# Queries and keys of retention heads 2 to 4 as seven half-width products, and retention's angle tables made a stage later

## The chip, the cores and the metric

The kernel runs on one core of a Trainium2 chip. The metric is device time in microseconds, from the start of the program to the end of its last instruction on the core. Times before are from three runs; the profile is one further execution, recorded by the hardware profiler.

## The reference

One layer of a decoder trunk, float32, batch 1, 512 positions, model width 1024. What matters here:

```python
h = rms_norm(x, norm_mix)
proj = h @ w_in
rq, rk, rv, rg, cq, ckv, krope, gr, gm = jnp.split(proj, offsets, axis=-1)

rq = rope(rq.reshape(B, S, RET_HEADS, RET_QK_DIM), pos)
rk = rope(rk.reshape(B, S, RET_HEADS, RET_QK_DIM), pos) * (RET_QK_DIM ** -0.5)
rv = rv.reshape(B, S, RET_HEADS, RET_V_DIM)
ro = retention(rq, rk, rv)
ro = rms_norm(ro, ret_norm.reshape(RET_HEADS, RET_V_DIM)).reshape(B, S, RET_V_W)
a_ret = (ro * jax.nn.silu(rg)) @ w_br
...
mo = causal_block_attention(q, k, v).reshape(B, S, MLA_V_W)
a_mla = mo @ w_bm
mixed = jax.nn.sigmoid(gr) * a_ret + jax.nn.sigmoid(gm) * a_mla
x = x + mixed @ w_o
```

Retention has 4 heads with queries and keys of 256 and values of 512 columns; `rope` turns each head's query and key by position: with the first 128 and last 128 of its columns called x1 and x2 it gives x1 cos - x2 sin and x2 cos + x1 sin. Cosine and sine depend on position and column alone and are one pair of 128 x 512 tables for all four heads. The other branch is latent attention with 8 heads. After `mixed @ w_o` come an MLP of width 4096 and a gated embedding, which the change doesn't touch.

## The kernel before

**Products.** Everything is held transposed: 128 channels on the partitions, 512 positions along the free axis. A product in float32 is made of three matmuls in a reduced format (`mm3`, L290 to L295): each operand is split into a high half `h` (a copy on ScalarE, rounded) and a low half `l` (VectorE, the rest), and low x high, high x low and high x high are added up in PSUM. All matmuls are recorded at one line, L167, so the profile's names tell them apart: `rq` and `rk` are the query and key products, `rv` and `rg` value and gate, `bm` the attention branch's output, `br` the retention branch's.

**Weights** come in chunks of 128 x 1024 (512 KB). SyncE issues the load into one of 6 raw tiles (`wr_...`), ScalarE makes the high half `wh_...` (L260), VectorE the low half `wl_...` (L264). There are 3 buffers for each half, so the halves of a chunk can be made only when TensorE has done the chunk three before it. One chunk is converted ahead of its use.

**Seven products for eight.** Values and gates are made two heads at a time by a scheme that multiplies two 2 x 2 block matrices with seven block products in place of eight. The blocks are halves of the depth (2 x 512 channels) and of positions (2 x 256) on the one side, halves of the depth and the two heads on the other. Its seven products have numbers 1, 7, 2, 6, 5, 4, 3. The activations' sums and differences, `XS[p]`, are made once (`x_operand`, tiles `sx`, `sy` and halves such as `s60h`). The sums and differences of weights are made by transfers: the fifth and seventh product's raw tile is loaded, and a second chunk is added to it by an accumulating transfer that GpSimd issues; the sixth and fourth product's is made in the seventh's tile by a further accumulating transfer each. `seven_out` puts the result together: a ScalarE copy out of PSUM after products 1, 7 and 6, a VectorE addition after 2, 5 and 4, and product 3 is the last block itself.

**Queries and keys** are made by `ret_qk` for each head separately: two chunks for the query and two for the key, each 8 x 3 matmuls with 512 columns and 128 output channels. After each, two VectorE products with the tables (512 columns each), after the second a difference and a sum, then the split in halves (`rqx`, `rqy`, `rkx`, `rky`).

**Tables.** Retention's are made early in the attention stage, between the statistics of the first pair of heads and the first head's factor: `ret_angles` (nine VectorE instructions on `tra` and `trk`, L466 to L477) and `ret_sincos` (two Sin and a Square on ScalarE, L485 to L487, and one VectorE instruction, L488), with the positions as loaded at the start.

**Order.** The steps of the kernel are a list, written out by hand. TensorE does them in that order. The framework's scheduler places the instructions of VectorE and ScalarE among those of earlier and later steps; each engine then works through its own list strictly in order. Heads go in pairs. In a pair: the first head's query and key, values and gates of both heads in seven products each, scores and attention of the first head, then (`ret_gated`, `ret_turned`, `branch_r`) its output times gate, 16 transposes on TensorE (`ot`), whose results are split in the halves `rog..h` (ScalarE, L308) and `rog..l` (VectorE, L311), and the branch product `br` from these. In the profile's names heads count from 0: `rog02l` is the low half of block 2 of the first head. The first head's `br` works on four blocks for each of its outputs; a first chunk of the second head's key stood between `ot` and `br`.

Of the kernel before, what the change touches and what calls it, by code (L numbers as in the profile page):

```python
# [37 lines left out]
P = 128  # L38
S = 512
# [12 lines left out]

C_ID, C_MASK, C_IND, C_INVR, C_INVM, C_SGN, C_N = 0, 128, 256, 260, 261, 262, 263

NDYN, NKEEP, NW, NRAW, NDRAW, AHEAD, PREP, EARLY, PAD = 45, 16, 3, 6, 4, 1, 3, 5, 104
GROUPS = DFF // 1024


# [12 lines left out]
def chunk_specs():  # L71
# [30 lines left out]
        for key, name in (("bm", "w_bm"), ("o", "w_o"), ("pg", "w_ple_gate")):  # L102
            add((key, n), name, full, _rng(n * P, P))
    for h in range(RH):
        for key, o in (("rq", O_RQ), ("rk", O_RK)):
            for n in range(2):
                add((key, h, n), "w_in", full, _rng(o + h * RQK + n * P, P))
        for k in range(4):
            add(("br", h, k), "w_br", _rng(h * RV, RV), _rng(2 * k * P, 2 * P))

    for kb in range(2):
        for fb in range(2):
            for q in range(RH // 2):
# [33 lines left out]
def trunk_layer(ctx: ExitStack, tc: tile.TileContext, xT, pT, pos, gains, const, decay, wstream, outT):  # L147
# [314 lines left out]


    def trig(name, posf, inv):
        ang, kf, c_, s_ = T(name + "a"), T(name + "k"), T(name + "c"), T(name + "s")
        TS(ang, posf, inv, None, op0=ALU.mult)  # L466
# [10 lines left out]
        TS(ang, ang, 3.1415925, -3.1415925, op0=ALU.min, op1=ALU.max)  # L477
        return ang, c_, s_
# [12 lines left out]
    def angles():  # L491
        posf = T("posf")
        nc.vector.tensor_copy(posf, posi)
        V["posf"] = posf
        V["am"] = trig("tm", posf, cst[:, C_INVM:C_INVM + 1])

    def tables():
        V["cm"], V["sn"] = sincos(*V["am"])

    def ret_angles():  # L500
        V["ar"] = trig("tr", V["posf"], cst[:, C_INVR:C_INVR + 1])

    def ret_sincos():
        V["cr"], V["sr"] = sincos(*V["ar"])
# [239 lines left out]
    def seven_out(c, p, ps, name):  # L744

        if p in (1, 7, 6):
            to = {1: 11, 7: 22, 6: 21}[p]
            c[to] = (T if to == 21 or name[0] == "c" else Z)(f"{name}{to}")
            ACT(c[to], ps, AF.Copy, scale=1.0 if p == 7 else -1.0)
            return None  # L750
        if p == 3:
# [53 lines left out]
    def ret_qk(w, h, key, n):  # L805
# [5 lines left out]
        if n == 0:  # L811
            d[key] = (a, b)
        else:
            a0, b0 = d[key]
            TT(a0, a0, a, op=ALU.subtract)
# [389 lines left out]
    for n in range(8):  # L1205
        step(("bm", n), branch_m, n)
        if n < 6:
            step(None, norm_x, 2 + n)
        if n == 3:
            step(None, x_operand, 7)  # L1210
    for p in (1, 2, 4):
        step(None, x_operand, p)
    def qk(h, key, n):
        step((key, h, n), ret_qk, h, key, n)

    def branch(h, *ks):
        for k in ks if h >= 0 else ():
            step(("br", h, k), branch_r, h, k)

    for q in range(RH // 2):  # L1220
        h = 2 * q
        qk(h, "rq", 0)
        qk(h, "rq", 1)
        if q:
            step(None, ret_turned, h - 1)
        qk(h, "rk", 0)
        branch(h - 1, 0)
        qk(h, "rk", 1)
        branch(h - 1, 1)
        for kind in ("rv", "rg"):  # L1230

            for p in (1, 7, 2, 6, 5, 4, 3):
                for c in range(2):
                    step(("sw", (kind, q), p, c), ret_seven, kind, q, p, c)
                if (kind, q) == ("rv", 0) and p in (1, 7, 2):
                    step(None, x_operand, {1: 6, 7: 5, 2: 3}[p])
                if (kind, p) == ("rv", 1):
                    branch(h - 1, 2)
                    if q:
                        step(None, ret_scores, h)  # L1240
                elif (kind, p) == ("rv", 6):
                    branch(h - 1, 3)
                    if not q:
                        step(None, ret_scores, h)
                elif (kind, p) == ("rg", 1):
                    step(None, ret_attend, h)
                elif (kind, p) == ("rg", 6):
                    qk(h + 1, "rq", 0)
                elif (kind, p) == ("rg", 4):
                    step(None, ret_gated, h)  # L1250
        qk(h + 1, "rq", 1)
# [131 lines left out]
```

## Time and profile before

| | us |
|---|---|
| median of 3 runs | 1105.74 (1105.18 to 1105.89) |
| the profiled execution | 1106.31 |
| its span | 1104.5 |
| TensorE busy | 1093.7 |
| VectorE busy | 711.1 |
| ScalarE busy | 541.1 |
| GpSimd busy | 89.9 |

The span is from the first to the last instruction that the profiler recorded. PE is TensorE, DVE VectorE, ACT ScalarE, POOL GpSimd, SP SyncE. A matmul's recorded duration overlaps with the next one's, so distances between starts tell what it takes. A row of the timeline has the start, the duration, engine, line, operation, output and inputs, shapes; a square bracket at its end tells the engine's idle time just before and what ended it. A row of the waits tells who waited for whom: total us, times, longest. A row of transfers ends with the median us from issue to landing.

### The profile page before, as it was taken

Reading aid. Unit: us, or ns where it says so; the run is one execution under the profiler, and the core shown is the slowest. Engines: PE = TensorE matmul, PEld = TensorE weight load, DVE = VectorE, ACT = ScalarE, POOL = GpSimd, SP = SyncE. Lnnn points to the kernel's source line nnn. Section 1 sums busy time; section 2 is a strip of 40 time slices with the busy share of each in tenths; the row PEclk is TensorE's granted clock in tenths of the full one; section 3 lists DMA queues with packets and bytes.
Section 4 is the critical chain, followed back from the end, with each engine's and each line's share of the span. In section 5 each row is a group of like instructions: output and inputs, shape, how many; then the busy total and the mean of one; then the engine's idle time right before and its main releaser. Section 6 shows DMA issues by size and latency. Waiting matters only on the chain.

```text
span 1104.5 us, 13845 instructions
## 1 busy us (share of the span) xinstructions
PE 1093.7 (99%) x5137; PEld 910.8 (82%) x5137; DVE 711.1 (64%) x1135; ACT 541.1 (49%) x785; POOL 89.9 (8%) x121
## 2 busy tenths in 40 slices
PE   9999999999999999999999999999999999999998
PEld 6778888888888888888888887888888888888887
DVE  7697677556774654656465577555556656658685
ACT  7647556444456545355654634434544444445542
POOL 0000000001111001121100100010100100101000
PEclk9999999999999999999999999999999999999999
DMA  7242231366789635488864944693765765738511
GB/s 258 72 120 87 72 106 54 128 208 205 207 194 246 195 143 171 116 202 205 209 207 115 268 142 158 193 276 103 181 172 150 184 182 136 190 116 219 147 54 58
DMA packets 59860, 178.02 MB, mean 161 GB/s; under 512 B 7376, under 2 KB 8784, under 8 KB 59536
## 3 DMA queue, kind: packets, MB, share of 16 engines
q1 hardware_dynamic: 45168, 129.66, 34.6%
q0 software_dynamic: 14480, 47.46, 21.6%
q8 instruction: 40, 0.66, 0.2%
q14 instruction: 28, 0.23, 0.1%
q10 hardware_dynamic: 144, 0.03, 0.0%
HBM read 157.97 MB, written 17.04 MB: 158 GB/s over the span
## 4 chain that ended last, share of the span: by engine, by line
PE 92%; DVE 4%; ACT 1%; issue 1%; DMA 1%; SPq 0%; DVEq 0%; ACTq 0%
PE up L167 16%; PE dn L167 14%; PE rv L167 7%; PE rg L167 7%; PE br L167 6%; PE pg L167 4%; PE gr L167 4%; PE rk L167 4%; PE bm L167 4%; PE rq L167 4%; PE wo L167 4%; PE gm L167 3%; PE ro L167 2%; PE sc L167 2%; PE pcq L167 1%; PE rs L167 1%
## 5 line engine op out<-in xcount | busy, mean ns | idle before, releaser
L167 PE MATMUL dn<-wh_dn,cl 128*128 128x512 f32 x224 | 87.2, 389 | 0.0
L167 PE MATMUL dn<-wh_dn,ch 128*128 128x512 f32 x224 | 87.1, 389 | 0.0
L167 PE MATMUL dn<-wl_dn,ch 128*128 128x512 f32 x224 | 87.1, 389 | 0.0
L260 ACT ACTIVATE wh_dn<-wr_dn 128x1024 fp32r<-128x1024 f32 x32 | 34.0, 1062 | 75.4 <-PE up L167 54.3
L260 ACT ACTIVATE wh_up<-wr_up 128x1024 fp32r<-128x1024 f32 x32 | 33.9, 1061 | 57.7 <-PE up L167 29.3
L264 DVE TENSOR_TENSOR wl_dn<-wr_dn,wh_dn 128x1024 fp32r<-128x1024 f32 x32 | 39.0, 1220 | 27.5 <-ACT wh_dn L260 27.5
L264 DVE TENSOR_TENSOR wl_up<-wr_up,wh_up 128x1024 fp32r<-128x1024 f32 x32 | 39.1, 1222 | 18.6 <-ACT wh_up L260 18.6
L167 PEld LDWEIGHTS dn<-wh_dn,cl 128*128 128x128 f32 x224 | 42.0, 188 | 8.8
L167 PEld LDWEIGHTS dn<-wh_dn,ch 128*128 128x128 f32 x224 | 42.0, 188 | 8.7
L982 DVE SCALAR_TENSOR_TENSOR f<-up,bcx 128x512 f32<-128x512 f32 x32 | 20.6, 685 | 44.4 <-PE up L167 44.4
L167 PEld LDWEIGHTS dn<-wl_dn,ch 128*128 128x128 f32 x224 | 42.0, 188 | 8.6
L260 ACT ACTIVATE wh_dn<-dr_dn 128x1024 fp32r<-128x1024 f32 x24 | 25.4, 1060 | 42.5 <-PE up L167 29.4
L260 ACT ACTIVATE wh_rg<-wr_rg 128x1024 fp32r<-128x1024 f32 x28 | 29.6, 1059 | 31.1 <-PE rg L167 12.1
L260 ACT ACTIVATE wh_rv<-wr_rv 128x1024 fp32r<-128x1024 f32 x28 | 29.6, 1058 | 30.6 <-PE rv L167 11.0
L222 POOL DMA_DIRECT2D dr_dn<-wstream x24 | 21.1, 890 | 289.4 <-DMA dr_dn<-wstream 165.0
L264 DVE TENSOR_TENSOR wl_dn<-dr_dn,wh_dn 128x1024 fp32r<-128x1024 f32 x24 | 29.3, 1222 | 22.4 <-ACT wh_dn L260 22.4
L264 DVE TENSOR_TENSOR wl_rg<-wr_rg,wh_rg 128x1024 fp32r<-128x1024 f32 x20 | 24.5, 1226 | 23.6 <-ACT wh_rg L260 23.6
L264 DVE TENSOR_TENSOR wl_rv<-wr_rv,wh_rv 128x1024 fp32r<-128x1024 f32 x20 | 24.4, 1223 | 18.0 <-ACT wh_rv L260 18.0
L1040 DVE TENSOR_TENSOR d<-d,dn 128x1024 f32<-128x1024 f32 x24 | 29.2, 1219 | 6.5 <-PE dn L167 6.5
L264 DVE TENSOR_TENSOR wl_br<-wr_br,wh_br 128x1024 fp32r<-128x1024 f32 x16 | 19.5, 1221 | 19.3 <-ACT wh_br L260 19.3
L260 ACT ACTIVATE wh_br<-wr_br 128x1024 fp32r<-128x1024 f32 x16 | 16.9, 1059 | 21.0 <-issue 12.8
L871 ACT ACTIVATE rt<-br 128x512 f32<-128x512 f32 x24 | 13.9, 593 | 25.9 <-PE br L167 25.9
(1819 smaller groups left out, 3440.7 us busy)
## 6 DMA issues: line engine op xcount, KB each, us to landing
wr_up<-wstream SPq DMA_DIRECT2D x32, 512.0 KB, 4.1
wr_dn<-wstream SPq DMA_DIRECT2D x32, 512.0 KB, 3.4
dr_dn<-wstream POOLq DMA_DIRECT2D x24, 512.0 KB, 7.6
wr_rv<-wstream SPq DMA_DIRECT2D x20, 512.0 KB, 4.4
wr_rg<-wstream SPq DMA_DIRECT2D x20, 512.0 KB, 5.3
wr_rv<-wstream POOLq DMA_DIRECT2D x16, 512.0 KB, 6.3
wr_rg<-wstream POOLq DMA_DIRECT2D x16, 512.0 KB, 7.4
wr_br<-wstream SPq DMA_DIRECT2D x16, 512.0 KB, 3.9
```

What stands on the lines that cost most here:

```text
L167: return tc.keep_in_program_order(nc.tensor.matmul(*a, **k))
L222: nc.gpsimd.dma_start(raw, chunk(("w", blk, kb, fb, c)), accum_op=ALU.add)
L260: i = ACT(hi, raw, AF.Copy, scale=sign)
L264: TT(lo, raw, hi.bitcast(F32), op=ALU.subtract)
L871: ACT(t, ps, AF.Copy)
L982: STT(u[:, i], ps[:, i], 0.0, V["bcx2"], op0=ALU.max, op1=ALU.mult)
L1040: TT(to, to, dps[p], op=ALU.add if sign > 0 else ALU.subtract)
```

## The change

Two things are changed.

First, queries and keys of the heads 1, 2 and 3 (heads 2 to 4 counted from one) are made by the scheme of seven as well: the two "columns" of the block matrix are now the head's query and key, 256 channels each. A product is 4 depth blocks x 2 output halves x 3 = 24 matmuls with 256 columns, with the weights as the stationary operand and `XS[p]` as the moving one. So a head has seven weight chunks of 24 short matmuls where it had four of 24 long ones, 5 plain and 4 accumulating loads where it had 4 plain ones, and the rotation is done in blocks of 256 positions (`ret_qk7`): per block one VectorE product of 512 columns and four operations of 256. Head 0 stays as it was. Steps are in a new order: the second head's seven products are spread among the gate products, and the last three stand before `ret_turned`; then both branch steps of the first head follow directly.

Second, `ret_angles` and `ret_sincos` move from the attention stage to that of `branch_m`, after its third and fifth output, with the positions loaded once more. The tables stand in one tile, `tab`. The pool of work tiles has 43 in place of 45.

```diff
-        for key, o in (("rq", O_RQ), ("rk", O_RK)):
+        for key, o in (("rq", O_RQ), ("rk", O_RK)) if h == 0 else ():
...
+            for h in range(1, RH):
+                add(("w", ("qk", h), kb, fb, 0), "w_in", _rng(kb * S, S), _rng((O_RQ, O_RK)[fb] + h * RQK, RQK))
...
     def ret_angles():
-        V["ar"] = trig("tr", V["posf"], cst[:, C_INVR:C_INVR + 1])
+        again, posf = dyn.tile([P, S], I32, tag="t", name="posr"), T("posrf")
+        nc.sync.dma_start(again, pos.partition_broadcast(P))
+        nc.vector.tensor_copy(posf, again)
+        V["ar"] = trig("tr", posf, cst[:, C_INVR:C_INVR + 1])
...
+    def ret_qk7(w, h, p):
+
+        ch, d = CHAIN[p], R[h]
+        if p in (1, 7, 2):
+            qkps[ch] = B(f"qk{h}{p}")
+        ps = qkps[ch]
+        for o in range(2):
+            for k in range(4):
+                mm3(ps[:, o * 256:o * 256 + 256], cut(w, k * 256 + o * P), XS[p][k], p in (1, 7, 2) and o + k == 0,
+                    o == 1 and k == 3, skip_group_check=True)
+        done = seven_out(d.setdefault("qk", {}), p, ps, f"qk{h}_")
+        if not done:
+            return
+        blk, t = done
+        key, cs = ("rq", "rk")[blk % 10 - 1], slice(256 * (blk // 10 - 1), 256 * (blk // 10))
+        a, b = T(f"{key}a{h}{blk}"), T(f"{key}b{h}{blk}")
+        lo_, hi_ = slice(0, 256), slice(256, 512)
+        TT(a.rearrange("p (k c) -> p k c", k=2), t.rearrange("p (k c) -> p k c", k=2), V["tab"][:, :, cs], op=ALU.mult)
+        TT(b[:, lo_], t[:, lo_], V["tab"][:, 1, cs], op=ALU.mult)
+        TT(b[:, hi_], t[:, hi_], V["tab"][:, 0, cs], op=ALU.mult)
+        first = key not in d
+        if first:
+            d[key] = (T(f"{key}u{h}"), T(f"{key}v{h}"))
+        u, v = d[key]
+        TT(u[:, cs], a[:, lo_], a[:, hi_], op=ALU.subtract)
+        TT(v[:, cs], b[:, lo_], b[:, hi_], op=ALU.add)
+        if not first:
+            d[key] = (split(u, f"{key}x{h}"), split(v, f"{key}y{h}"))
...
-    step(None, ret_angles)
-    step(None, ret_sincos)
     step(None, head_factor, 0)
...
+        if n in (2, 4):
+            step(None, ret_angles if n == 2 else ret_sincos)
...
+        if q:
+            qk(h, 1, 7, 2, 6)
+            step(None, ret_turned, h - 1)
+            qk(h, 5)
+            branch(h - 1, 0)
+            qk(h, 4, 3)
+            branch(h - 1, 1)
...
+        seven("rg", q, 7, 2, 6)
+        qk(h + 1, 1, 7)
+        seven("rg", q, 5)
+        qk(h + 1, 2)
+        seven("rg", q, 4)
+        step(None, ret_gated, h)
+        qk(h + 1, 6)
+        seven("rg", q, 3)
+        qk(h + 1, 5, 4, 3)
         step(None, ret_turned, h)
-        qk(h + 1, "rk", 0)
-        branch(h, 0)
-        qk(h + 1, "rk", 1)
-        branch(h, 1)
+        branch(h, 0, 1)
         step(None, ret_scores, h + 1)
```

Two places show what the change does to the engines' own lists. The first is VectorE around the transposes `ot` and the branch product `br` of head 0. In these names `z` and `o` are gate and output, `wl_...` a low half of weights, `rog00l` to `rog03l` the low halves that `br` multiplies, and `rqa`, `rqb`, `rqu`, `rqv`, `rka`, `rkb`, `rku`, `rkv` steps of the rotation. Before:

```order
L264 TENSOR_TENSOR wl_br_0_3991<-wr_br_0_3988,wh_br_0_3990 128x1024
L809 TENSOR_TENSOR rqa_3938<-rq_3913,trs 128x512
L810 TENSOR_TENSOR rqb_3939<-rq_3913,trc 128x512
L815 TENSOR_TENSOR rqa_3784<-rqa_3784,rqa_3938 128x512
L816 TENSOR_TENSOR rqb_3785<-rqb_3785,rqb_3939 128x512
L311 SCALAR_TENSOR_TENSOR rog00l<-ot_3952,gn,rog00h 128x512
L306 TENSOR_TENSOR rqx1l<-rqa_3784,rqx1h 128x512
L311 SCALAR_TENSOR_TENSOR rog01l<-ot_3961,gn,rog01h 128x512
L306 TENSOR_TENSOR rqy1l<-rqb_3785,rqy1h 128x512
L264 TENSOR_TENSOR wl_rk_1_4026<-wr_rk_1_4023,wh_rk_1_4025 128x1024
L311 SCALAR_TENSOR_TENSOR rog02l<-ot_3970,gn,rog02h 128x512
L311 SCALAR_TENSOR_TENSOR rog03l<-ot_3979,gn,rog03h 128x512
```

After, from the first weight half of `br` on; ahead of it stand, since the fifth of head 1's products, `qk_22`'s sum and its rotation (six rows as from `qk_21` to `rqv` here):

```order
L266 TENSOR_TENSOR wl_br_0_4103<-wr_br_0_4100,wh_br_0_4102 128x1024
L763 TENSOR_TENSOR qk_21_3977<-qk_21_3977,qk_3797 128x512
L266 TENSOR_TENSOR wl_br_1_4184<-wr_br_1_4181,wh_br_1_4183 128x1024
L847 TENSOR_TENSOR rqa_4085<-qk_21_3977,tab 128x512
L848 TENSOR_TENSOR rqb_4086<-qk_21_3977,tab 128x256
L849 TENSOR_TENSOR rqb_4086<-qk_21_3977,tab 128x256
L854 TENSOR_TENSOR rqu_3898<-rqa_4085 128x256
L855 TENSOR_TENSOR rqv_3899<-rqb_4086 128x256
L313 SCALAR_TENSOR_TENSOR rog00l<-ot_4145,gn,rog00h 128x512
L308 TENSOR_TENSOR rqx1l<-rqu_3898,rqx1h 128x512
```

and on to the fourth block:

```order
L313 SCALAR_TENSOR_TENSOR rog01l<-ot_4154,gn,rog01h 128x512
L308 TENSOR_TENSOR rqy1l<-rqv_3899,rqy1h 128x512
L847 TENSOR_TENSOR rka_4130<-qk_3764,tab 128x512
L848 TENSOR_TENSOR rkb_4131<-qk_3764,tab 128x256
L849 TENSOR_TENSOR rkb_4131<-qk_3764,tab 128x256
L854 TENSOR_TENSOR rku_4052<-rka_4130 128x256
L855 TENSOR_TENSOR rkv_4053<-rkb_4131 128x256
L266 TENSOR_TENSOR wl_br_2_4224<-wr_br_2_4221,wh_br_2_4223 128x1024
L308 TENSOR_TENSOR rkx1l<-rku_4052,rkx1h 128x512
L308 TENSOR_TENSOR rky1l<-rkv_4053,rky1h 128x512
L313 SCALAR_TENSOR_TENSOR rog02l<-ot_4163,gn,rog02h 128x512
L313 SCALAR_TENSOR_TENSOR rog03l<-ot_4172,gn,rog03h 128x512
```

Between `rog01l` and `rog03l` stood one row of the query, one of weights and `rog02l`; now the key's last rotation, a chunk of weights and both key splits stand there too.

The second place is ScalarE in front of retention's first query product, which multiplies `xn0` to `xn7` (`gb` is the other branch's gate, a Sigmoid; `s60h` and `s61h` belong to `XS[6]`). Before:

```order
L260 ACTIVATE wh_rq_1_2970<-wr_rq_1_2968 128x1024
L305 ACTIVATE s60h<-sx_2792 128x512
L305 ACTIVATE xn6h<-xr_2843 128x512
L696 ACTIVATE gb_2856<-gb_2856 128x512
L260 ACTIVATE wh_rk_0_3005<-wr_rk_0_3003 128x1024
L305 ACTIVATE xn7h<-xr_2887 128x512
L305 ACTIVATE s61h<-sx_2793 128x512
```

After:

```order
L262 ACTIVATE wh_rk_0_3008<-wr_rk_0_3006 128x1024
L307 ACTIVATE xn6h<-xr_2842 128x512
L492 ACT_TABLE_LOAD
L492 ACTIVATE tab<-tra 128x512
L493 ACTIVATE tab<-tra 128x512
L494 ACTIVATE tab<-tab 128x512
L705 ACT_TABLE_LOAD
L705 ACTIVATE gb_2859<-gb_2859 128x512
L307 ACTIVATE xn7h<-xr_2890 128x512
L307 ACTIVATE s61h<-sx_2792 128x512
```

`xn6h` stood before the key's weight half and stands behind it now, and the two Sins, the Square and two table loads stand between it and `xn7h`.

More of the change, by code (lines that the diff above doesn't have):

```diff
@@ L53 @@
 C_ID, C_MASK, C_IND, C_INVR, C_INVM, C_SGN, C_N = 0, 128, 256, 260, 261, 262, 263
-NDYN, NKEEP, NW, NRAW, NDRAW, AHEAD, PREP, EARLY, PAD = 45, 16, 3, 6, 4, 1, 3, 5, 104
+NDYN, NKEEP, NW, NRAW, NDRAW, AHEAD, PREP, EARLY, PAD = 43, 16, 3, 6, 4, 1, 3, 5, 104
 GROUPS = DFF // 1024
@@ L464, in trig @@
     def trig(name, posf, inv):
-        ang, kf, c_, s_ = T(name + "a"), T(name + "k"), T(name + "c"), T(name + "s")
+        ang, kf = T(name + "a"), T(name + "k")
+        if name == "tr":
+            V["tab"] = dyn.tile([P, 2, S], F32, tag="tab", name="tab", bufs=1)
+            c_, s_ = V["tab"][:, 0], V["tab"][:, 1]
+        else:
+            c_, s_ = T(name + "c"), T(name + "s")
         TS(ang, posf, inv, None, op0=ALU.mult)
@@ L493, in angles @@
         nc.vector.tensor_copy(posf, posi)
-        V["posf"] = posf
         V["am"] = trig("tm", posf, cst[:, C_INVM:C_INVM + 1])
@@ L747, in seven_out @@
             to = {1: 11, 7: 22, 6: 21}[p]
-            c[to] = (T if to == 21 or name[0] == "c" else Z)(f"{name}{to}")
+            c[to] = (Z if to != 21 and name[0] == "z" else T)(f"{name}{to}")
             ACT(c[to], ps, AF.Copy, scale=1.0 if p == 7 else -1.0)
@@ L817, in ret_qk @@
             d[key] = (split(a0, f"{key}x{h}"), split(b0, f"{key}y{h}"))
+    qkps = {}
+    def ret_qk7(w, h, p):
[25 more added lines that the diff above has]
+            d[key] = (split(u, f"{key}x{h}"), split(v, f"{key}y{h}"))
     def ret_scores(h):
@@ L1212, in trunk_layer, with qk, seven @@
         step(None, x_operand, p)
-    def qk(h, key, n):
-        step((key, h, n), ret_qk, h, key, n)
+    def qk(h, *ps):
+        for p in ps:
+            step(("sw", ("qk", h), p, 0), ret_qk7, h, p)
+    def seven(kind, q, *ps):
+        for p in ps:
+            for c in range(2):
+                step(("sw", (kind, q), p, c), ret_seven, kind, q, p, c)
     def branch(h, *ks):
-        for k in ks if h >= 0 else ():
+        for k in ks:
             step(("br", h, k), branch_r, h, k)
@@ L1221, in trunk_layer @@
         h = 2 * q
-        qk(h, "rq", 0)
-        qk(h, "rq", 1)
         if q:
+            qk(h, 1, 7, 2, 6)
             step(None, ret_turned, h - 1)
[L1226 to L1251, printed above, removed]
+            qk(h, 5)
+            branch(h - 1, 0)
+            qk(h, 4, 3)
+            branch(h - 1, 1)
+            seven("rv", q, 1)
+            branch(h - 1, 2)
+            step(None, ret_scores, h)
+            seven("rv", q, 7, 2, 6)
+            branch(h - 1, 3)
+        else:
+            for key in ("rq", "rk"):
+                for n in range(2):
+                    step((key, h, n), ret_qk, h, key, n)
+            for p, x in ((1, 6), (7, 5), (2, 3)):
+                seven("rv", q, p)
+                step(None, x_operand, x)
+            seven("rv", q, 6)
+            step(None, ret_scores, h)
+        seven("rv", q, 5, 4, 3)
+        seven("rg", q, 1)
+        step(None, ret_attend, h)
+        seven("rg", q, 7, 2, 6)
[7 more added lines that the diff above has]
+        qk(h + 1, 5, 4, 3)
         step(None, ret_turned, h)
-        qk(h + 1, "rk", 0)
-        branch(h, 0)
-        qk(h + 1, "rk", 1)
-        branch(h, 1)
+        branch(h, 0, 1)
         step(None, ret_scores, h + 1)
```

## The prediction

> **What bounds the kernel now.** I read the page first: busy time by engine and the chain of work that ended last.
>
> ```profile
> PE 1093.7 (99%) x5137; PEld 910.8 (82%) x5137; DVE 711.1 (64%) x1135; ACT 541.1 (49%) x785; POOL 89.9 (8%) x121
> ...
> PE 92%; DVE 4%; ACT 1%; issue 1%; DMA 1%; SPq 0%; DVEq 0%; ACTq 0%
> ```
>
> TensorE is busy for 1093.7 of the span's 1104.5 us. So the time changes in two ways only: TensorE gets less work, or it gets (or loses) stalls. The next view, the busy time between 204 and 667 us (from the end of attention through retention, where nearly all of the change lies), shows a TensorE without a gap; the waits of TensorE show that what stalls there are lie elsewhere. Four of them are of this change's first place, the attention stage:
>
> ```profile
> 204.00:667.00 463.00, 463.00 (x2132) 387.19 (x2131) 281.97 (x422) 230.94 (x346) 56.89 (x76) 1.00 0.67 187
> ```
>
> ```profile
> PE sc L167 <- ACT sqk L525: 0.8, 1, 0.8
> PE gm L167 <- DVE mx L642: 0.6, 1, 0.6
> PE pt0a L167 <- DVE p L651: 0.6, 1, 0.6
> ```
>
> The first row's columns are the stretch, its length, the busy time of PE, PEld, DVE, ACT and POOL, the granted clock (1.00) and the DMA share (0.67). In retention VectorE is busy for 282 of 463 us and ScalarE for 231: they have room in the mean. What counts is whether they are late at one moment.
>
> **Term 1, fewer cycles on TensorE.** Per head 4 chunks of 24 products over 512 columns become 7 chunks of 24 over 256. The timeline gives the distance between starts of both kinds: the first and the 25th matmul of `rq`, and 13 starts of the last gate product, which has 256 columns.
>
> ```profile
> 275.18 0.39 PE L167 MATMUL rq<-xn0h,wl_rq 128*128 128x512 f32 x1
> ...
> 280.62 0.39 PE L167 MATMUL rq<-xn0h,wl_rq 128*128 128x512 f32 x1
> ```
>
> ```profile
> 1097.06 0.28 PE L167 MATMUL pg<-x3g0h,wl_pg 128*128 128x256 f32 x1
> ...
> 1098.50 0.28 PE L167 MATMUL pg<-x3g4h,wl_pg 128*128 128x256 f32 x1
> ```
>
> (280.62 - 275.18)/24 = 0.227 us, and (1098.50 - 1097.06)/12 = 0.120 us, each with its own weight load. A head costs 96 x 0.227 = 21.8 us now and 168 x 0.120 = 20.2 us after: -1.6 us, not the -12.5% that seven for eight suggests, since the shorter matmul loses more of its time between two. Three heads: **-4.9 us**. Bounds: 0, if each of the 504 short ones started 0.01 us later than these rows have it, and -4.9, which I take. [...]
>
> **Term 2, the angle block leaves the attention stage.** Nine VectorE instructions and three of ScalarE stand between head 0's scores and their softmax:
>
> ```profile
> 83.82 0.48 DVE L466 TENSOR_SCALAR tra<-posf,cst 128x512 f32<-128x512 f32 x1
> ...
> 88.63 0.43 DVE L477 TENSOR_SCALAR tra<-tra 128x512 f32<-128x512 f32 x1
> 90.77 0.29 DVE L642 CUSTOM_DVE_ANT_0 p<-sc,kf 128x128 f32<-128x128 f32 x1 [1.70 <-ACT kf L611]
> ```
>
> ```profile
> 89.10 0.63 ACT L485 ACTIVATE trs<-tra 128x512 f32<-128x512 f32 x1 [5.21 <-DVE tra L477]
> ...
> 90.16 0.58 ACT L611 ACTIVATE kf<-pbk 128x512 f32<-128x512 f32 x1
> ```
>
> `kf`, on which the maximum at 90.77 waits, stands on ScalarE behind the Sin of 89.10. Without the block the softmax is 3 to 4 us earlier, and the waits of `sc`, `gm` and `pt0a` above, 0.8 + 0.6 + 0.6 = 2.0 us, lose their cause. Bounds: -2.0 and 0; in the changed order the low half of the next gate chunk stands behind `k3l`, a wait that can take some of it back. I take **-1.1**, about the middle.
>
> **Term 3, the angle block arrives in front of retention.** Its nine VectorE instructions go between those of the other branch's stage, whose VectorE is half idle; they cost nothing while TensorE's operands stay ahead. The ScalarE part does not fit so well. It brings two table loads (Sin, and Sigmoid back), and the order puts table, Sin, Sin, Square, table and a Sigmoid between `xn6h` and `xn7h`, the last operand of retention's first product. Now:
>
> ```profile
> 240.44 1.28 ACT L696 ACT_TABLE_LOAD   x1
> 241.74 0.63 ACT L696 ACTIVATE gb<-gb 128x512 f32<-128x512 f32 x1
> ...
> 271.47 0.62 ACT L305 ACTIVATE xn6h<-xr 128x512 fp32r<-128x512 f32 x1
> 271.99 0.61 ACT L696 ACTIVATE gb<-gb 128x512 f32<-128x512 f32 x1
> 275.43 1.06 ACT L260 ACTIVATE wh_rk<-wr_rk 128x1024 fp32r<-128x1024 f32 x1 [2.83 <-PE bm L167]
> 276.40 0.61 ACT L305 ACTIVATE xn7h<-xr 128x512 fp32r<-128x512 f32 x1
> ```
>
> ```profile
> 277.67 0.68 DVE L306 TENSOR_TENSOR xn7l<-xr,xn7h 128x512 fp32r<-128x512 f32 x1
> ```
>
> ```profile
> 280.16 0.39 PE L167 MATMUL rq<-xn7l,wh_rq 128*128 128x512 f32 x1
> ```
>
> `xn7l` ends at 278.35, and TensorE takes it at 280.16: 1.8 us of cover. After, `wh_rk` still starts at 275.43 (it waits for the last `bm` product), and `xn6h` now stands behind it, to 277.0. Then table 1.28, two Sins (the second 0.52 after the first), Square, table 1.28, Sigmoid: 276.9 -> 278.2 -> 279.9 -> 281.2 -> 281.8, so `xn7h` ends at about 282.4 and `xn7l`, with a product of VectorE before it, at 283.2. TensorE wants it at 280.16: **+3.0 us** (2 if the ScalarE starts overlap better, 4 if VectorE's own queue there, five instructions, comes on top).
>
> **Term 4, the transposed output of heads 1 and 3 is wanted at once.** Now a whole `rk` chunk lies between the transposes `ot` and the branch product `br`, which needs all four of `rog0`..`rog3`:
>
> ```profile
> 394.66 1.91 PE L167 MATMUL ot<-cst,o 128*128 128x128 f32 x16
> 396.32 0.48 PE L167 MATMUL rk<-xn0h,wl_rk 128*128 128x512 f32 x1
> ...
> 401.86 0.39 PE L167 MATMUL br<-rog00h,wl_br 128*128 128x512 f32 x1
> ```
>
> ```profile
> 395.47 0.68 DVE L810 TENSOR_TENSOR rqb<-rq,trc 128x512 f32<-128x512 f32 x1
> 396.06 0.68 DVE L815 TENSOR_TENSOR rqa<-rqa,rqa 128x512 f32<-128x512 f32 x1
> ...
> 397.26 0.74 DVE L311 SCALAR_TENSOR_TENSOR rog00l<-ot,gn,rog00h 128x512 fp32r<-128x512 f32 x1
> ...
> 399.79 1.22 DVE L264 TENSOR_TENSOR wl_rk<-wr_rk,wh_rk 128x1024 fp32r<-128x1024 f32 x1
> 400.92 0.74 DVE L311 SCALAR_TENSOR_TENSOR rog02l<-ot,gn,rog02h 128x512 fp32r<-128x512 f32 x1
> 401.58 0.74 DVE L311 SCALAR_TENSOR_TENSOR rog03l<-ot,gn,rog03h 128x512 fp32r<-128x512 f32 x1
> ```
>
> `rog03l` ends at 402.32, 6.0 us after the transposes' end (396.32), and costs nothing, since `br` reaches its fourth operand only some 2 us after 401.86. After, `br` follows `ot` directly. I put the new VectorE order on these durations: 0.60 for a 512 column product (396.06 - 395.47), 1.13 for a weight's low half (400.92 - 399.79), 0.66 for a `rog` low half (401.58 - 400.92). For a 256 column product the trace has 0.34:
>
> ```profile
> 273.42 0.42 DVE L731 TENSOR_TENSOR sx<-xr,sx 128x256 f32<-128x256 f32 x1
> 273.76 0.75 DVE L735 TENSOR_TENSOR sx<-xr,sx 128x256 f32<-128x256 f32 x2
> ```
>
> Take the start of `ot` as 0. The last two seven-step chunks (5.8 us) stand before it, so VectorE may begin with the fifth's result at -5.8 + 0.2 = -5.6 (rq ends at 394.66 now and VectorE answers at 394.86, 0.2 later). From there it has no gap: sum and rotation of the first block 2 x 0.60 + 4 x 0.34 = 2.56, `wl_br` 1.13, the next sum 0.60, `wl_br` 1.13, the rotation of the second block 0.60 + 4 x 0.34 = 1.96: to +1.8. Then `rog00l`, `rqx1l`, `rog01l`, `rqy1l` (2.5, to +4.3); then, still ahead of `rog02l`, the third block's rotation 1.96, `wl_br` 1.13, `rkx1l` and `rky1l` 1.2 (to +8.6); then `rog02l`, and `rog03l` from +9.3 to +10.0. The first `br` output could be done at 1.66 + 12 x 0.227 = 4.4; with its last operand at 10.0 it ends at 10.0 + 0.2 + 2 x 0.227 = 10.6. A stall of **6.2 us**, in head 1 and in head 3 alike: **+12.4 us**. Bounds: 0 if those instructions get done by +3.7, 6.9 if a ScalarE half (`rog02h` stands behind `rky1h` there) comes later still. I take the middle value, since every duration in it has a row of the same shape.
>
> **Terms at or near nothing.** Head 2's `rog` halves have 2.9 us of product before `br`, and on ScalarE `rog11h` stands behind a weight half that waits for an accumulating transfer: 0 to 0.8, I take **+0.4**. Per head three more weight conversions, 3 x 1.06 us on ScalarE and 3 x 1.22 on VectorE, lie beside 20 us of products (a head's first chunks have over half of both engines' time idle). The transfers: per head 4 loads before; 5 loads and 4 accumulating ones after.
>
> ```profile
> wr_rg<-wstream SPq DMA_DIRECT2D x20, 512.0 KB, 5.3
> ...
> wr_rg<-wstream POOLq DMA_DIRECT2D x16, 512.0 KB, 7.4
> ```
>
> ```profile
> q1 hardware_dynamic: 45168, 129.66, 34.6%
> q0 software_dynamic: 14480, 47.46, 21.6%
> ```
>
> By q1 a plain 0.524 MB takes 0.346 x 1104.5 / 129.66 x 0.524 = 1.54 us of the 16 engines, by q0 an accumulating one 2.63: 5 x 1.54 + 4 x 2.63 = 18.2 us a head for 6.2 now. The stretch above had a DMA share of 0.67, so there is room; what can be late is a chain of transfers. I take 0, bounds 0 and 6 (rival C).
>
> **Sum** on the profiled execution: -4.9 - 1.1 + 3.0 + 12.4 + 0.4 = +9.8. It took 1106.3 us (the span of 1104.5 and 1.8 around it), 0.6 above the median of the runs, 1105.74; the forecast goes by the median: 1105.7 + 9.8 = **1115.5 us**.
>
> **Rivals.**
>
> A, faster. Heads 1 and 3 have their operands in time: VectorE's backlog runs ahead of the products that feed it, and `rog03l` is done by +3.7, when `br` needs it. For it: VectorE is busy only 282 of 463 us. Against: 14.9 us of VectorE's work stand between the fifth product's end and `rog03l`, and TensorE gives it 5.8 + 3.7 = 9.5. Then terms 1, 2 and 3 are left: 1105.7 - 4.9 - 1.1 + 3.0 = 1102.7, and 1099.7 if term 3's cover holds too. Chance 0.09.
>
> B, half the stall. VectorE's backlog is gone when `ot` ends, and `rog03l` is ready as far behind the transposes as now, 6.0 us: `br`'s first output ends at 6.0 + 0.2 + 0.45 = 6.7 after them, 3.9 later than the 2.7 of its own. Twice 3.9 in place of 12.4: 1110.9. Against it: two more `wl_br` and a whole rotation stand before `rog03l`. Chance 0.17.
>
> C, the transfers. The fourth `qk` product's weights are accumulated into the tile of the sixth's, so their load starts when the sixth's halves are made. In heads 2 and 4 that is about 2.4 us after the second product's end (1.06 + 1.22 and the answers); the fourth starts 2 x 5.44 (a gate product of 24 x 0.227) and 2 x 2.88 later than that end, 16.6 in all. Less 2.4 for its own halves and 7.4 for the landing, 4.4 us are to spare. A landing twice as long, 14.8, is 3.0 late in each: 1115.5 + 6.0 = 1121.5. For it: nine transfers stand where four stood, four of them on the slow queue. Against: 7.4 is the median of transfers that already run between others of their kind. Chance 0.08.
>
> D, dearer table loads. In the trace a load takes 1.28 us, and the next instruction starts 1.30 after it (240.44 to 241.74). If each new load stalls the engine by as much again, term 3 gets 2 x 1.3 more: 1118.1. Chance 0.05. [...]
>
> **How the numbers follow.** Forecast 0.57, A 0.09, B 0.17, C 0.08, D 0.05, and 0.04 that the losses of terms 3 and 4 and gains of 1 and 2 cancel. Range: 1107.5 (B without term 3, 1107.9) to 1121.0 (D with term 4 at 6.9 each, 1119.5, and part of C): A and most of C are left out, some 0.16. Of this kernel a measurement can tell 0.2% (2.2 us) from no change: faster than 1103.5 is A, 0.09; within is the cancelling case, 0.04; slower the rest, 0.87.
>
> **What would show it.** In the changed profile: 504 `qk` matmuls at starts 0.120 apart; waits of TensorE `br` on VectorE's `rog` low halves of heads 1 and 3, 5 to 7 us each; a wait of `rq` on `xn7` of 2 to 4 us; the waits of `gm` and `pt0a` gone; three table loads where one stood between 230 and 290 us. Wrong would be: a `br` that starts without a wait behind `ot` (then A), `qk` starts over 0.13 apart (term 1 falls), or a TensorE that waits for the halves of `qk` weights (then C).

## The result: 1122.45 us, 1.5% slower

The changed kernel takes 1122.45 us (median of four runs, 1121.82 to 1123.69); the kernel before took 1105.82 beside it. The ratio is 1.0152, with an interval of 1.0139 to 1.0165. The forecast was 1115.5 with a range of 1107.5 to 1121.0: the direction was right, and the time lies above the range.

### The profile after

The page's busy times and chain, and the same stretch as before, 204 to 667 us (length, then busy time of PE, PEld, DVE, ACT and POOL, granted clock, DMA share):

```profile
PE 1096.8 (98%) x5353; PEld 920.0 (82%) x5353; DVE 730.2 (65%) x1178; ACT 558.1 (50%) x805; POOL 100.6 (9%) x133
...
PE 43%; DVE 1%; issue 1%; ACT 0%; DVEq 0%
```

```profile
204.00:667.00 463.00, 448.30 (x2265) 381.00 (x2265) 288.73 (x448) 241.61 (x359) 67.03 (x87) 0.99 0.73 197
```

The chain can be followed back over 45% of the span only, so it says nothing of retention. The stretch does: TensorE stands still for 14.7 of 463 us where it had no gap, and its granted clock is no longer 1.00. The span is 1121.0 us (1104.5 before). TensorE's busy time went up by 3 us although the products got shorter: part of them ran slower. The waits, in the order of the view:

```profile
PE br L169 <- ACT rog02h L310: 3.2, 1, 3.2
PE br L169 <- ACT rog22h L310: 3.2, 1, 3.2
PE rq L169 <- ACT xn7h L307: 2.5, 1, 2.5
...
PE qk L169 <- DVE wl_qk L266: 1.4, 1, 1.4
...
PE br L169 <- DVE rog11l L313: 0.8, 1, 0.8
```

The first matmul of three stages, before and after, divides the difference:

```profile
231.63 0.40 PE L167 MATMUL bm<-mos0h,wl_bm 128*128 128x512 f32 x1
...
296.94 0.39 PE L167 MATMUL rv<-wh_rv,xn0l 128*128 128x512 f32 x1
...
667.68 0.39 PE L167 MATMUL wo<-mix0h,wl_o 128*128 128x512 f32 x1
```

```profile
229.78 0.40 PE L169 MATMUL bm<-mos0h,wl_bm 128*128 128x512 f32 x1
...
298.50 0.39 PE L169 MATMUL rv<-wh_rv,xn0l 128*128 128x512 f32 x1
...
683.79 0.39 PE L169 MATMUL wo<-mix0h,wl_o 128*128 128x512 f32 x1
```

| us | up to `bm` | `bm` to `rv` | `rv` to `wo` | `wo` to the end |
|---|---|---|---|---|
| before | 231.63 | 65.31 | 370.74 | 436.82 |
| after | 229.78 | 68.72 | 385.29 | 437.21 |
| difference | -1.85 | +3.41 | +14.55 | +0.39 |

**Behind `ot` of head 1.** These are TensorE's rows there:

```profile
405.56 1.91 PE L169 MATMUL ot<-cst,o 128*128 128x128 f32 x16
407.44 0.50 PE L169 MATMUL br<-rog00h,wl_br 128*128 128x512 f32 x1
408.72 0.51 PE L169 MATMUL br<-rog00l,wh_br 128*128 128x512 f32 x1 [0.78 <-DVE rog00l L313]
...
413.93 0.80 PE L169 MATMUL br<-rog02h,wl_br 128*128 128x512 f32 x1 [3.22 <-ACT rog02h L310]
415.51 0.80 PE L169 MATMUL br<-rog02l,wh_br 128*128 128x512 f32 x1 [0.79 <-DVE rog02l L313]
416.10 0.63 PE L169 MATMUL br<-rog02h,wh_br 128*128 128x512 f32 x1
416.53 0.63 PE L169 MATMUL br<-rog03h,wl_br 128*128 128x512 f32 x1
...
419.94 0.44 PE L169 MATMUL br<-rog01h,wh_br 128*128 128x512 f32 x1
```

and the end of VectorE's list that the prediction had put on durations:

```profile
415.38 0.74 DVE L313 SCALAR_TENSOR_TENSOR rog03l<-ot,gn,rog03h 128x512 fp32r<-128x512 f32 x1
```

`rog03l` ends at 416.12, 10.56 us after the start of `ot`; 10.0 were worked out. The longest wait, 3.22 us, is one for a high half, which ScalarE makes:

```profile
412.15 0.63 ACT L307 ACTIVATE rkx1h<-rku 128x512 fp32r<-128x512 f32 x1 [2.72 <-DVE rku L854]
...
413.21 0.67 ACT L310 ACTIVATE rog02h<-ot,gn 128x512 fp32r<-128x512 f32 x1
```

`rog02h` stands on ScalarE behind the key's high halves, and the first of these waits 2.72 us for VectorE's rotation. So VectorE's list makes TensorE wait twice: by way of ScalarE, and by its own low halves. The four waits of head 1 add up to 5.1 us, 1.9 of them for low halves.

Behind the wait of 3.22 us the starts are 0.43 us apart up to 419.94, in place of 0.227 (416.10 to 416.53): TensorE goes at about half its clock for 6 us after it has its operands again. Between 404 and 428 us the granted clock is 0.86, around head 3's `ot` too; both rows are shown with the first experiment. At full clock the first output would have ended 0.6 after `rog03l`, at 416.7, and not at 417.81, where the next one begins; five further slow starts, up to 419.94, add 1.0. So head 1 loses 6.5 us to the operands (416.7 less 407.44 + 2.72) and some 2.2 to the clock, head 3 in the same way 6.1 and 1.5.

**In front of retention's first product.** ScalarE's list and TensorE's wait:

```profile
275.18 1.28 ACT L492 ACT_TABLE_LOAD   x1
276.47 0.63 ACT L492 ACTIVATE tab<-tra 128x512 f32<-128x512 f32 x1
...
278.31 1.28 ACT L705 ACT_TABLE_LOAD   x1
...
280.14 0.61 ACT L307 ACTIVATE xn7h<-xr 128x512 fp32r<-128x512 f32 x1
```

The wait is 2.5 us, with 0.3 more for `xn7l` and what lies around a restart 3.4.

**Head 2, a wait that was not expected.** GpSimd's list before and after, around the reloads of the second head's values:

```profile
420.89 0.55 POOL L801 DMA_DIRECT2D rv12l<-v2d  x1
421.90 0.55 POOL L801 DMA_DIRECT2D rv13l<-v3d  x1 [0.46 <-PE rs L167]
```

```profile
429.74 0.55 POOL L810 DMA_DIRECT2D rv12l<-v2d  x1
439.17 0.90 POOL L224 DMA_DIRECT2D wr_qk<-wstream  x1 [8.88 <-DVE wl_qk L266]
439.74 0.89 POOL L810 DMA_DIRECT2D rv13l<-v3d  x1
```

```profile
445.58 0.63 ACT L307 ACTIVATE rv13h<-rv13l 128x512 fp32r<-128x512 f32 x1 [2.53 <-DMA rv13l<-v3d]
```

An accumulating load of `qk` weights waits 8.9 us on GpSimd for a weight half, and the last reload, which needs nothing, stands behind it: 10.0 us after the third one, where it was 1.0. ScalarE in turn waits for it, and behind that stand the copies of the second head's attention. They end some 2.5 us later than they would, by ScalarE's wait in the last row; `ret_gated` and the sixth product's weight half follow, and TensorE waits 1.4 us for that, and a little later 0.8 for `rog11l`.

### The profile page after: what moved, and what is told of

It reads as the page before. It is cut to its first block, busy times and chain, and to the rows that moved or that the text cites. A ratio compares the mean times of both kernels' runs of the same rounds, so it can differ in the third digit from the quotient of the medians.

```text
span 1121.0 us, 14372 instructions
## 1 busy us (share of the span) xinstructions
PE 1096.8 (98%) x5353; PEld 920.0 (82%) x5353; DVE 730.2 (65%) x1178; ACT 558.1 (50%) x805; POOL 100.6 (9%) x133
## 5 line engine op out<-in xcount | busy, mean ns | idle before, releaser
L266 DVE TENSOR_TENSOR wl_dn<-dr_dn,wh_dn 128x1024 fp32r<-128x1024 f32 x24 | 29.4, 1223 | 22.4 <-ACT wh_dn L262 22.4
L262 ACT ACTIVATE wh_qk<-wr_qk 128x1024 fp32r<-128x1024 f32 x21 | 22.3, 1063 | 19.7 <-DMA wr_qk<-wstream 7.3
```

Source lines behind the costliest of these rows:

```text
L262: i = ACT(hi, raw, AF.Copy, scale=sign)
L266: TT(lo, raw, hi.bitcast(F32), op=ALU.subtract)
```

## Experiments

**e1, does the clock cost anything of its own?** Matmuls whose result nobody uses fill the time behind `ot`.

```diff
+    def keep_busy(h):
+        ps = B(f"fill{h}")
+        for i in range(22):
+            MM(ps, xn[0][0][:, 0:P], xn[0][0], start=i == 0, stop=i == 21)
...
         step(None, ret_turned, h)
+        step(None, keep_busy, h)
         branch(h, 0, 1)
```

> The changed kernel (1122.45 us) with 22 matmuls of 512 columns put between the transposes of heads 1 and 3 and their branch product; they work on operands that are ready and nobody uses their result, so TensorE is busy for 22 x 0.227 = 5.0 us where it waited 3.2 us in one piece. Nothing that rog0 to rog3 need changes, so rog03l ends when it ended. Theory (half the clock after the wait): the slow matmuls go, branch products end 2.0 us earlier in head 1 and 1.3 in head 3, 1119.0 us in all, and the granted clock of the kernel is 1.00. Rival (the slow stretch has another cause, for instance the traffic of that moment): the clock stays at 0.993 and the time at 1122.4 or above. If the whole loss of the two places were waiting for operands, the time would not move either.

Measured: 1120.2 us (1119.52 to 1120.55), ratio to before 1.013 (1.0115 to 1.0145). The windows of `ot` and `br` in head 1 and head 3, of the changed kernel and of this one:

```profile
404.00:428.00 24.00, 18.93 (x84) 14.63 (x83) 13.34 (x23) 9.18 (x15) 3.41 (x5) 0.86 0.60 163
600.00:624.00 24.00, 19.36 (x91) 15.21 (x90) 13.44 (x24) 10.14 (x16) 3.10 (x4) 0.86 0.47 105
```

```profile
272.00:290.00 18.00, 15.44 (x61) 12.02 (x60) 12.59 (x21) 10.87 (x14) 3.07 (x5) 0.91 0.83 247
404.00:428.00 24.00, 23.03 (x122) 19.59 (x121) 14.84 (x25) 10.82 (x17) 5.41 (x9) 1.00 0.66 175
600.00:624.00 24.00, 22.92 (x116) 19.06 (x115) 14.83 (x27) 10.92 (x17) 3.43 (x4) 1.00 0.59 130
```

With 5 us more work in each place, the kernel is 2.25 us faster, and the clock there is 1.00. So the slow stretch is a cost of its own, and it comes from TensorE's standing still. The gain is less than the 3.4 expected; in this profile a slow stretch stands at another place, 272 to 290 us (0.91, where the changed kernel had 1.00), behind the wait for `xn7`, of the same length in both. It costs 1.2 us, about what the gain falls short by.

**e2, the order.** One step is moved.

```diff
+        step(None, ret_turned, h)
         qk(h + 1, 5, 4, 3)
-        step(None, ret_turned, h)
         branch(h, 0, 1)
```

> The changed kernel with one step moved: in heads 1 and 3 the transposes stand before the last three of the second head's seven products instead of behind them, so 8.6 us of products lie between them and the branch product. Theory (order on VectorE and ScalarE): both stalls and the slow clock behind them go, 8.7 + 7.6 = 16.3 us, 1106.2 us (1104 to 1108). Rival (VectorE has too much work there in any order): the rotation is late instead and the scores wait for it, 3 us or more per pair come back, 1112 or above.

Measured: 1107.54 us (1105.96 to 1108.54), ratio 1.0014 (1.0004 to 1.0023): 14.9 us less, within the theory's bounds. No wait of `br` is left in heads 1 and 3. So the late operands of `br` were an effect of the list and not of VectorE's load, whose work is the same. What is lost against the 16.3: head 2's wait for the weight half is 2.2 us here in place of 1.4, with a slow stretch behind it (granted clock 0.95 between 436 and 470 us; 4 us in all at that place, 1.6 before).

**e3, GpSimd's queue.**

```diff
             if h == 1:
-                nc.gpsimd.dma_start(lo.bitcast(F32), src)
+                nc.sync.dma_start(lo.bitcast(F32), src)
```

> The changed kernel with the four reloads of the second head's values issued by SyncE instead of GpSimd. Theory (queue): the fourth reload stood on GpSimd's list behind an accumulating load that waits for a weight half, so the second head's attention was copied out late, and with it the gate, the weight half of the third head's sixth product (1.4 us wait of TensorE) and, by a late accumulating load, rog11h (0.8): 1.6 to 2.7 us, 1119.8 to 1120.9. Rival (the transfers as such are slow because accumulating ones share the engines): no change, 1122.4.

Measured: 1122.53 us (1122.06 to 1123.12), ratio 1.0152 (1.0137 to 1.0167). The wait for the sixth product's weight half is gone, `br` of head 2 has lost 0.6 of its 1.1 us; the time is the same. In the profile, slow stretches at the other places make up for it: the windows 272 to 290, 404 to 428 and 600 to 624 have clocks of 0.91, 0.86 and 0.86, and what the three places lose beyond their work went from 19.7 to 22.9 us. The granted clock was 0.992 in all four executions (the changed kernel has 0.993 to 0.994 in the four of the result, and 0.992 in e9), so it is not this one execution alone. Why moved times should bring more slow clock, this run does not tell; e10 asks again without the other waits.

**e4, the place of the tables.**

```diff
-        if n in (2, 4):
-            step(None, ret_angles if n == 2 else ret_sincos)
+        if n in (0, 1):
+            step(None, ret_angles if n == 0 else ret_sincos)
```

> The changed kernel with the angle tables made after the first and second output of the other branch instead of the third and fifth. Theory (the ScalarE list ahead of xn7): the two table loads and three table instructions lie 20 us before retention's first product; the wait for xn7 of 2.9 us shrinks to 0.4 to 1.2 us, since the scale of the last x block still stands behind a weight half on VectorE; 1119.5 to 1120.2 us. Rival (a stage of so much ScalarE work is late wherever the table loads stand): 1122 or above.

Measured: 1122.23 us (1121.49 to 1123.24), ratio 1.015 (1.0135 to 1.0165): by the time the rival holds. By the profile the wait for `xn7h` fell from 2.5 to 1.4 us, less than worked out, and the place's loss from 3.4 to 2.1; heads 1 and 3 lose 0.7 more there; that this is the clock's is the author's estimate (0.994 over this execution, 0.993 over the changed kernel's). This run cannot tell the tables' share from the clock's.

**e5, all of it mended.** The edits of e2, e3 and e4, and `XS[7]` made after the other branch's seventh output in place of its fourth, by which the scheduler puts the last x blocks in front of the weight half again.

```diff
-        if n == 3:
+        if n == 6:
             step(None, x_operand, 7)
```

> The changed kernel with all three causes taken away: the transposes ahead of the last three of the second head's seven products (as in e2_turn), the reloads of the second head's values on SyncE (as in e3_queue), the tables after the first and second output of the other branch, and there the sums XS[7] behind the stage instead of in it, so that on VectorE the last x blocks stand ahead of the weight half again. Theory: what is left is the gain of the shorter products, 4.9 us, and of the attention stage, 1.85, less some 0.5 at head 2's branch product: 1105.7 - 6.3 = 1099.4 (1098.5 to 1101). No wait of TensorE between 230 and 667 us above 0.5 and a granted clock of 1.00. Rival (each wait taken away comes back at the next late operand, and the slow clock with it): 1103 or above.

Measured: 1100.04 us (1099.31 to 1101.41), ratio **0.9949** (0.9936 to 0.9963): 5.7 us faster than the kernel before and 22.4 faster than the changed one. Two stretches of retention, with head 1's `br` in the first and head 2's in the second:

```profile
400.00:430.00 30.00, 30.00 (x156) 25.87 (x155) 20.69 (x37) 13.29 (x21) 4.83 (x7) 1.00 0.70 197
430.00:470.00 40.00, 39.88 (x263) 36.39 (x262) 29.93 (x56) 22.69 (x39) 6.58 (x9) 1.00 0.70 180
```

Up to `bm` it takes 229.51 us, from `bm` to `rv` 65.30, to `wo` 366.53: against before -2.1, 0.0 and -4.2. In the last 0.46 us are still lost at head 2's `br` (its first output takes 3.19 us, 12 x 0.227 without a wait), so the seven products give 4.7 us. As expected no wait above 0.5 us is left between 230 and 667 us, and the granted clock there is 1.00. In front of retention's first product the run has two edits at once; e4, with the tables' place alone, still lost 2.1 us there; with `XS[7]` moved as well nothing is lost.

**e6, the seven products alone,** with the edits of e2 and e3 and the tables in the attention stage.

```diff
+    step(None, ret_angles)
+    step(None, ret_sincos)
     step(None, head_factor, 0)
...
-        if n in (2, 4):
-            step(None, ret_angles if n == 2 else ret_sincos)
```

> Part one alone, mended as in e2_turn and e3_queue: the seven products of heads 2 to 4, with the tables made in the attention stage as before. Theory (a product of 256 columns costs 0.120 us a matmul, and nothing else of it is on TensorE's path): 1105.7 - 4.9 + 0.5 = 1101.3 (1100.3 to 1102). Rival (three more weight chunks a head, and accumulating loads, cost elsewhere what the products save): 1104 or above.

Measured: 1107.02 us (1105.43 to 1107.93), ratio 1.0008 (0.9999 to 1.0016). By the time the rival would hold; the profile has the loss at another place than it says. From `bm` to `rv` it takes 65.31 and from `rv` to `wo` 366.53 us, the same as e5: there the products keep their gain. But `bm` begins at 236.66, 5.0 us later than before. The waits name the attention stage:

```profile
PE pt0a L169 <- DVE p L658: 2.0, 1, 2.0
PE st L169 <- ACT sums L594: 1.9, 1, 1.9
```

Both waits, shorter than 2.1 us, are followed by the slow clock. Behind the wait for `sums`, which ends at 78.58, the starts are 0.42 us apart:

```profile
80.00 0.63 PE L169 MATMUL gm<-xg0h,wh_gm 128*128 128x512 f32 x1
80.42 0.63 PE L169 MATMUL gm<-xg1h,wl_gm 128*128 128x512 f32 x1
```

The granted clock is 0.89 from 68 to 84 us and 0.79 from 100 to 108 (0.996 over the whole execution, 1.000 in the kernel before), so a good part of the 5.0 us is the clock's. The tables back in their step did not bring the old order back: in the kernel before, ScalarE makes `sums` at 75.41, ahead of a weight half (`wh_kq`), and here at 77.96, behind it. Why the scheduler placed the instructions there differently was not tested; the table tile is another, and the pool has 43 tiles. So this run does not measure part one alone over the whole span; it does for retention.

**e7, the tables alone,** in the kernel before.

```diff
-    step(None, ret_angles)
-    step(None, ret_sincos)
     step(None, head_factor, 0)
...
+        if n in (2, 4):
+            step(None, ret_angles if n == 2 else ret_sincos)
```

> Part two alone: the kernel before with the tables made after the third and fifth output of the other branch. Theory: 1.85 us less in the attention stage, 3.4 more at retention's first product, and in some executions a slow clock behind that wait: 1107.2, up to 1108.8. Rival (the wait at xn7 belongs to the seven products' other load, not to the tables): 1103.9.

Measured: 1113.01 us (1111.54 to 1115.45), ratio 1.0068 (1.0054 to 1.0081). Part two alone costs 7 us, and neither theory had the size. In the profile (an execution of 1112.01 us) the attention stage gains 3.5 us (`bm` at 228.14), and `bm` to `rv` takes 8.7 more: 5.5 at the wait for `xn7h`, and most of the rest behind it, where the granted clock between 272 and 290 us is 0.81. The wait, the instruction that is late, and SyncE's list:

```profile
PE rq L167 <- ACT xn7h L305: 5.3, 1, 5.3
```

```profile
280.48 0.75 DVE L712 SCALAR_TENSOR_TENSOR xr<-xr,gn,rbc 128x512 f32<-128x512 f32 x1 [3.37 <-DMA xr<-xT]
```

```profile
268.89 5.72 SPq L232 DMA_DIRECT2D wr_rv<-wstream  x2
...
275.49 0.33 SPq L711 DMA_DIRECT2D xr<-xT  x1
```

Here it is not ScalarE that is last but the load of the last x block: SyncE issued it at 275.49, behind two weight loads on which its list spent 5.7 us; in the kernel before it was issued at 267.80, between the two. By the profile it is the queue mechanism of head 2 on another engine; no run took this wait away alone. In the changed kernel VectorE had the last x block scaled at 279.40, and ScalarE came to it at 280.14, so ScalarE's list decided.

**e8, how long a wait brings the slow clock?** Twelve waits in the mended kernel, each a chain of 2 to 7 copies on ScalarE between two matmuls; the values of the products around them are not used.

```diff
+    def idle(i, k):
+        ps, t = B(f"ida{i}"), T(f"idt{i}", F32R)
+        MM(ps, xn[0][0][:, 0:P], xn[0][0], start=True, stop=True)
+        ACT(t, ps, AF.Copy)
+        for _ in range(k - 1):
+            ACT(t, t.bitcast(F32), AF.Copy)
+        MM(B(f"idb{i}"), t[:, 0:P], t, start=True, stop=True)
```

> The mended kernel of e5_mended with twelve waits put between products 7, 5 and 3 of values and gates: a matmul whose result ScalarE copies 2 to 7 times in a chain, and a matmul that reads the last copy, so that TensorE stands still for about 0.4 + 0.6 times the number of copies (1.6 to 4.6 us), and then goes on with operands that have long been ready. The values of these products are not used. Theory (a wait costs itself, and from a certain length on the clock is halved for some 3 us behind it): the short ones are followed by matmuls 0.227 apart, the long ones by matmuls 0.427 apart for some 3 us, and the same length at another place does the same. Rival (what counts is where the wait falls in a cycle of the clock's own): waits of one length between 2 and 3.5 us are followed by the slow clock at some places and not at others, and for stretches of different length.

Measured: 1175.74 us (one run), with waits of 2.78 to 5.7 us, longer than planned. Two of them, 3.07 and 3.39 us long:

```profile
575.73 0.50 PE L169 MATMUL idbrv<-idtrv 128*128 128x512 f32 x1 [3.07 <-ACT idtrv L910]
576.06 0.39 PE L169 MATMUL rg<-wh_rg,xn0l 128*128 128x512 f32 x1
```

```profile
559.37 0.50 PE L169 MATMUL idbrv<-idtrv 128*128 128x512 f32 x1 [3.39 <-ACT idtrv L910]
...
560.65 0.59 PE L169 MATMUL rv<-wl_rv,xn4h 128*128 128x512 f32 x1
561.04 0.63 PE L169 MATMUL rv<-wh_rv,xn4h 128*128 128x512 f32 x1
...
564.03 0.43 PE L169 MATMUL rv<-wh_rv,xn6l 128*128 128x512 f32 x1
```

The three shortest, up to 3.07, are followed by the full clock (1.00 in the 13 us around each); the nine from 3.39 on by the slow one (0.74 to 0.87 around the six up to 4.4 us; 0.980 over the whole run, half of whose lost clock these six make up). The slow stretch begins 1.3 us after the second of these waits, at 560.65, and ends at 564.03, 3.4 us later; over all nine places it is, by an estimate from the starts of the matmuls, some 3 to 6.4 us long and costs 1.4 to 2.9 us, with the matmul that ends the wait counted in. Waits of equal length differ in this (four waits of 4.4 us: 1.6, 2.9, 1.4 and 1.5). So within this run the length alone divides the waits, as the theory has it, and the stretches differ as the rival has it. The waits of 1.9 to 2.6 us in e2, e6, e9 and e10 are shorter than the three that the full clock followed here, and the slow clock came behind them; so over all runs the length alone does not decide. Whether a cycle of the clock's own does, as the rival has it, was not shown.

**e9, the changed kernel once more,** with no edit.

> The changed kernel itself once more, for a second profile of it: the waits of TensorE must be the same to 0.1 us. Theory (a fixed length decides): the slow stretches behind the branch products of heads 1 and 3 have the same length as in its first profile, and no slow stretch stands behind the wait for xn7. Rival (the clock's own cycle): their lengths differ by 1 us or more, and one may stand behind xn7.

Measured: 1123.63 us (one run). Its waits are those of the first profile to 0.1 us, except the one for `rog00l` (0.35 us, 0.78 in the first). But behind the wait for `xn7`, again 2.55 us long, a slow stretch stands now:

```profile
280.74 0.71 PE L169 MATMUL rq<-xn7h,wl_rq 128*128 128x512 f32 x1 [2.55 <-ACT xn7h L307]
...
282.57 0.63 PE L169 MATMUL rq<-xn0h,wl_rq 128*128 128x512 f32 x1
282.99 0.63 PE L169 MATMUL rq<-xn0l,wh_rq 128*128 128x512 f32 x1
```

So the second half of the rival's sentence holds: the same wait of 2.55 us is followed by the slow clock in one execution and not in the next. The first half does not: behind the `br` of heads 1 and 3 the stretches have the same length in both, to 0.1 us. A fixed length does not explain what stands behind `xn7`; what does was not shown.

**e10, the queue again,** in the mended kernel, with e3's edit undone.

```diff
             if h == 1:
-                nc.sync.dma_start(lo.bitcast(F32), src)
+                nc.gpsimd.dma_start(lo.bitcast(F32), src)
```

> The mended kernel of e5_mended (1100.04 us) with one of its changes undone: the reloads of the second head's values are issued by GpSimd again. In e3_queue that change took the wait for the third head's weight half away and the time stayed; there two slow stretches of the clock lay in the same execution. Here no other wait is left. Theory (the queue costs its waits): the wait for the sixth product's weight half is back with 1.4 to 2.3 us and rog11's with 0.6 more, and a slow clock behind it in some executions: 1102 to 1104. Rival (the late reload only takes the place of a wait that TensorE would have elsewhere): 1100 to 1100.8.

Measured: 1102.97 us (1102.03 to 1105.01), ratio to before 0.9975 (0.9966 to 0.9984): 2.9 us more than the mended kernel, as the theory has it. TensorE waits for `wl_qk` again:

```profile
PE qk L169 <- DVE wl_qk L266: 2.4, 1, 2.4
```

The wait for `rog11` that the theory had beside it is not back. The profiled execution took 1104.38 us, and its window of 436 to 456 us has a clock of 0.91. The other ten have a granted clock of 0.999 or 1.00 over the whole kernel, and the five at 1.00 took 1102.52 to 1103.00 us. So the late reload costs 2.9 us where nothing else is late, nearly all of it the wait, and some 4 where the slow clock follows.

## Why the prediction was wrong

| step | predicted | measured in the profile |
|---|---|---|
| 1, seven products | -4.9 | -4.7 (e5, e6) |
| 2, attention stage | -1.1 | -1.85 |
| 3, `xn7` | +3.0 | +3.4 |
| 4, `rog` operands, heads 1 and 3 | +12.4 | +12.6 |
| the clock behind them | not in the sum | +3.7 |
| head 2 | +0.4 | +2.7 |
| the rest (`ot`, from `wo` on) | 0 | some +0.6 |
| sum | +9.8 | +16.5 |

**The step that failed is the sum itself: it priced each wait at its own length.** "The time changes in two ways only", less work or stalls, left out a third way, the same work at half the clock, and so put it at nothing. Two waits of 3.2 us in one piece brought the slow clock, 3.7 us in the profile. e1 shows that it is a cost of its own; in e8 it came behind each wait from 3.39 us on. The working had the long wait in it, with `rog01l` done at +3.7 and `rog02l` begun at +8.6; but the clock in every window of before was 1.00, and no row showed what comes behind such a wait.

**The second is "head 2: 0 to 0.8", a term sized too small.** It looked for a late operand at ScalarE and named the accumulating transfer, which is there (`rog11l`, 0.8). It did not look at what such a load is put ahead of on GpSimd: the reload of `rv13`, for which TensorE waits 1.4 us at the sixth product. It read the new lists of VectorE and ScalarE row by row, and not GpSimd's. e10 measures the late reload at 2.9 us.

**Term 4** was right in mechanism and in size: the list of VectorE with durations from rows gave 10.0 for `rog03l`, and 10.56 and 10.1 were measured; the stalls are 6.5 and 6.1 for 6.2. The sign that it named, waits of 5 to 7 us for low halves, came in another form: the longest is for ScalarE's `rog02h`, which the prediction had only as an upper bound. The half us of head 1 comes from its start: the chain began 5.1 us ahead of `ot` and not 5.6, behind a weight half that itself came late. e2 shows that the order alone made it. Rivals A (the operands in time) and B (6.0 us after the transposes) are out.

**Term 1** was right: 0.120 us a matmul, and in e5 and e6 all but 0.2 of the 4.9 us is kept, so next to nothing is paid elsewhere for the 216 additional matmuls. **Term 3** was right within 0.4 us for the changed kernel: each table load took 1.28 us and the next instruction began 1.29 after its start, so rival D is out. Alone, in the kernel before, the same move cost 8.7 us for another reason (e7); the prediction did not consider SyncE's queue there. **Term 2** was sized too small by 0.75; the three waits that were to go are not all gone (0.6 is left at `gm`), but the stage gained as much.

**Rival C** is out in its form: no `qk` product of heads 2 and 4 waited. Accumulating loads of `qk` landed in 7.8 us, near the 7.4 assumed.

## What to carry to other kernels

When a list is written anew, go through every in-order queue, those of the engines that issue transfers too, and ask what now stands behind an instruction that waits; in this kernel a wait of GpSimd and one of SyncE were worth 2.9 and some 5 us, and one step's place 14.9. Price a stall of TensorE of 3.2 us or more at its length and, by these runs, 1.4 to 2.9 us on top; from 1.9 us on the extra can come. And a shorter product is only a gain where its operands' cover was counted in time and not in chunks: the step that vanished had been the cover of four others.

## What the runs showed of the hardware

Every wait of TensorE of 3.2 us or longer was followed by a lower granted clock, by the rows about half speed (512 columns 0.427 us apart, 0.227 otherwise): the 3.2 us ones of heads 1 and 3 in all four profiles that have them (windows of 0.86 in the changed kernel, e3 and e9; 0.994 over the whole of e4), the 5.3 us one of e7 (0.81), and nine in e8 (0.74 to 0.87 around six of them, 0.980 over the whole run), where the slow stretch is by estimate some 3 to 6.4 us long. After waits of 1.9 to 2.6 us it came in seven of nine cases (not behind `xn7` in the first profile of the changed kernel and in e2; there in e1, e3 and e9, and behind other waits in e2, e6 and e10). Three waits of 2.8 to 3.1 us in e8 were not followed by it (1.00 around each). So between 1.9 and 3.1 us length alone does not decide; what does is not shown here.
